# A weighted sum of expert outputs: twelve-token tiles in four buffers against sixteen-token tiles in three rooms

## The chip, the core and the metric

The kernel runs on one core of one Trainium2 chip. The metric is the device time of one execution in microseconds (us), the median of a few runs. The core has engines that compute, VectorE (DVE), ScalarE (ACT) and GpSimd (POOL), and SyncE (SP), which issues transfers. ACT and SP each issue transfers (DMAs) into a queue of their own, q10 and q1 in the profile; sixteen DMA engines serve both queues. TensorE (PE) has no work here.

## The reference

```python
batch, seq, hidden, n_experts, k = 16, 1024, 512, 8, 2
# expert_outputs: batch x seq x k x hidden, combine_weights: batch x seq x k, float32
def reference(expert_outputs, combine_weights):
    weights = combine_weights[..., np.newaxis]
    return np.sum(expert_outputs * weights, axis=2).astype(np.float32)
```

For each of 16,384 tokens, two rows of 512 numbers are scaled, each by its own weight, and added. A token is 4 KB of input and 2 KB of output: 67 MB are read and 33.5 MB written in all.

## The kernel before

The 16,384 tokens are spread over 128 partitions, 128 tokens each. The first 120 tokens of a partition are contiguous in memory (a pitch of 480 KB of input from one partition to the next, 240 KB of output); the last eight lie in a second block at the end of the tensors. `rows` (L34 to L38) hides that split.

The loop at L68 goes over eleven tiles: ten of 12 tokens and a last one of eight. Every tile takes one of four buffers of 12 tokens (`bufs=4`, 48 KB in each partition). Each tile is loaded by one DMA on SP (L75), so that a partition's part is one row of 48 KB; the first tile alone is cut into two tokens, moved in 4 KB rows, and ten. The result `ot` is written over the first half of the tile's own buffer, so that a buffer is free for the next load when its store has landed. SP therefore waits, before the load of tile g + 4, for the store of tile g.

There are three forms of the computation.

- Tiles 0 to 8: DVE alone multiplies the whole tile by its broadcast weights (L84), then adds the two halves (L85). ACT issues the store (L86).
- Tile 9: ACT scales the first half token by token (L92), DVE multiplies the second half (L107) and adds (L108). SP issues the store (L109).
- Tile 10, the last: token by token, ACT scales the first half (L92) and DVE does a multiply and add in one instruction (L96). SP issues the store.

Before all that ACT issues a small write of zeros to the output (`ahead`, L58), which the stores later cover, then the two loads of the weights (L62), and runs a one-element activation. The order on each engine is that of the program; a framework works out the semaphores for the waits. The queues serve their DMAs in order, and the sixteen DMA engines take from both queues.

Of the kernel before, what the change touches and what calls it, by code (L numbers as in the profile page):

```python
# [1 line left out]

# [4 lines left out]


@with_exitstack
def kernel(  # L10
    ctx: ExitStack,
    tc: tile.TileContext,
    expert_outputs: bass.AP,
    combine_weights: bass.AP,
    out: bass.AP,
):

    nc = tc.nc  # L20
    b, s, k, h = expert_outputs.shape
    assert k == 2
    n = b * s
    P = nc.NUM_PARTITIONS
    per = n // P
    assert per * P == n
    J, LAST = 12, 8
    main = per - LAST
    assert main % J == 0
    eo = expert_outputs.rearrange("b s k h -> (b s) (k h)")  # L30
    cw = combine_weights.rearrange("b s k -> (b s) k")
    o = out.rearrange("b s h -> (b s) h")

    def rows(x):  # L34

        a = x[0 : P * main, :].rearrange("(p t) f -> p t f", p=P)
        b = x[P * main : n, :].rearrange("(p t) f -> p t f", p=P)
        return lambda t, c: a[:, t : t + c, :] if t < main else b[:, t - main : t - main + c, :]  # L38

    eo, cw, o = rows(eo), rows(cw), rows(o)  # L40

    dt = mybir.dt.float32
    mult = mybir.AluOpType.mult
    add = mybir.AluOpType.add
    copy = mybir.ActivationFunctionType.Copy

    last = main // J

    wpool = ctx.enter_context(tc.tile_pool(name="w", bufs=1))
    ipool = ctx.enter_context(tc.tile_pool(name="in", bufs=4))  # L50

    wt = wpool.tile([P, per * k], dt)


    zt = wpool.tile([16, 128], dt)
    nc.vector.memset(zt, 0.0)  # L56
    first = out.rearrange("b s h -> (b s) h")[0 : P * main, :].rearrange("(q t) h -> q (t h)", q=16)
    ahead = nc.scalar.dma_start(out=first[:, 0:128], in_=zt)  # L58

    with tc.issue_after(ahead.ins):  # L60
        for t, c in ((0, main), (main, LAST)):
            nc.scalar.dma_start(  # L62
                out=wt[:, k * t : k * (t + c)].rearrange("p (t k) -> p t k", k=k), in_=cw(t, c)
            )
        warm = wpool.tile([P, 1], dt)
        nc.scalar.activation(out=warm, in_=nc.const_aps.tensor(1.0, (P, 1), dt), func=copy)  # L66

    for g in range(last + 1):  # L68
        et = ipool.tile([P, J, k * h], dt)

        ot = et.rearrange("p j f -> p (j f)")[:, 0 : J * h].rearrange("p (j f) -> p j f", f=h)
        t0, c = g * J, J if g < last else LAST

        for a, m in ((0, 2), (2, c - 2)) if g == 0 else ((0, c),):
            nc.sync.dma_start(  # L75
                out=et[:, a : a + m],
                in_=eo(t0 + a, m),
                max_dma_last_dim=k * h * 4 if g + a == 0 else None,
            )
        if g < last - 1:  # L80

            wb = wt[:, g * J * k : (g + 1) * J * k].unsqueeze(2).to_broadcast([P, J * k, h])
            ek = et.rearrange("p j (k h) -> p (j k) h", k=k)
            nc.vector.tensor_tensor(out=ek, in0=ek, in1=wb, op=mult)  # L84
            nc.vector.tensor_tensor(out=ot, in0=et[:, :, 0:h], in1=et[:, :, h : 2 * h], op=add)  # L85
            nc.scalar.dma_start(out=o(t0, c), in_=ot)  # L86
            continue


        for i in range(c):  # L90
            t = t0 + i
            nc.scalar.activation(  # L92
                out=et[:, i, 0:h], in_=et[:, i, 0:h], func=copy, scale=wt[:, 2 * t : 2 * t + 1]
            )
            if g == last:
                nc.vector.scalar_tensor_tensor(  # L96
                    out=ot[:, i, :],
                    in0=et[:, i, h : 2 * h],
                    scalar=wt[:, 2 * t + 1 : 2 * t + 2],
                    in1=et[:, i, 0:h],  # L100
                    op0=mult,
                    op1=add,
                )
        if g < last:
            w1 = wt.rearrange("p (t k) -> p t k", k=k)[:, t0 : t0 + c, 1:2]
            x1 = et[:, :, h : 2 * h]
            nc.vector.tensor_tensor(out=x1, in0=x1, in1=w1.to_broadcast([P, c, h]), op=mult)  # L107
            nc.vector.tensor_tensor(out=ot, in0=et[:, :, 0:h], in1=x1, op=add)  # L108
        nc.sync.dma_start(out=o(t0, c), in_=ot[:, 0:c])  # L109


# [1 line left out]
_INS = ['expert_outputs', 'combine_weights']  # L113
_OUTS = [((16, 1024, 512), 'float32')]


# [23 lines left out]
```

## Time and profile before

| what | value |
|---|---|
| runs | 239.13, 240.79, 239.16 us; median 239.16 |
| span of the profiled execution, first to last instruction | 237.34 us (no other time of that execution is listed) |
| median less that span | 1.82 us |
| DVE busy | 194.1 us in 29 instructions |
| ACT busy | 14.0 us in 22 instructions |
| moved | 100.80 MB in 3760 packets, 425 GB/s on the mean |
| load of 12 tokens, issue to landing | 29.9 us |
| store of 12 tokens on ACT's queue, issue to landing | 33.0 us |

A packet here is what a DMA engine moves in one go: the part of one partition in a DMA, 48 KB for a load of 12 tokens, 24 KB for its store. Each DMA of 128 partitions gives every one of the 16 engines eight packets. The DMA share is the busy time of the packets that start in a stretch, over 16 engines; in short stretches it swings, and can be over one, since a packet is counted whole where it starts.

### The profile page before, as it was taken

What the parts mean: (1) busy time and instruction counts of PE and PEld (TensorE: products, weight loads), DVE (VectorE), ACT (ScalarE), POOL (GpSimd) and SP (SyncE); (2) the same over time, 40 slices, a digit from 0 to 9 for tenths busy, and PEclk for the clock granted to TensorE, in tenths of its full rate; (3) what the DMA queues carried; (4) which work ended last, traced back from release to release, by engine and by line L of the source; (5) the groups of instructions that cost most, each with busy time, mean ns of one, the idle gap of its engine ahead of it and who ended that gap; (6) DMA issues with size and microseconds to landing.
All of it is one profiled execution on the core that took longest, in us unless ns stands there. A gap on an engine that the chain in (4) does not pass through costs nothing.

```text
span 237.3 us, 157 instructions
## 1 busy us (share of the span) xinstructions
DVE 194.1 (82%) x29; ACT 14.0 (6%) x22; POOL 0.2 (0%) x4
## 2 busy tenths in 40 slices
DVE  0008999999999999999999889969996998785710
ACT  2000000000000000000000000000000000740800
POOL 0000000000000000000000000000000000000000
DMA  7999999989899999999898999999998979999997
GB/s 289 452 474 398 398 448 480 398 356 505 352 443 435 427 464 464 398 398 530 348 514 348 447 418 443 464 464 398 398 522 348 522 344 451 464 398 442 406 434 309
DMA packets 3760, 100.80 MB, mean 425 GB/s; under 512 B 544, under 2 KB 688, under 8 KB 944
## 3 DMA queue, kind: packets, MB, share of 16 engines
q1 hardware_dynamic: 2144, 72.35, 71.0%
q10 hardware_dynamic: 1616, 28.45, 27.9%
HBM read 67.24 MB, written 33.56 MB: 425 GB/s over the span
## 4 chain that ended last, share of the span: by engine, by line
DMA 59%; DVE 34%; ACT 2%; ACTq 0%; DVEq 0%; issue 0%; SPq 0%
DMA out_dram<-et 29%; DMA et<-in_expert_outputs_dram 23%; DVE et L84 22%; DVE et L85 11%; DMA wt<-in_combine_weights_dram 7%; ACT et L92 2%; DVE et L96 1%; DVEq L135 0%; ACTq L135 0%; ACTq L58 0%; DVE zt L56 0%; DVEq L84 0%; SPq L75 0%; ACTq L92 0%
## 5 line engine op out<-in xcount | busy, mean ns | idle before, releaser
L84 DVE TENSOR_TENSOR et<-et,wt 128x12288 f32<-128x12288 f32 x9 | 116.6, 12955 | 24.1 <-DMA wt<-in_combine_weights_dram 17.5
L85 DVE TENSOR_TENSOR et<-et 128x6144 f32<-128x6144 f32 x9 | 59.0, 6557 | 0.3
L92 ACT ACTIVATE et<-et,wt 128x512 f32<-128x512 f32 x20 | 12.5, 708 | 208.6 <-DMA et<-in_expert_outputs_dram 208.6
L96 DVE SCALAR_TENSOR_TENSOR et<-et,wt 128x512 f32<-128x512 f32 x8 | 5.6, 746 | 3.9 <-ACT et L92 3.6
L107 DVE TENSOR_TENSOR et<-et,wt 128x6144 f32<-128x6144 f32 x1 | 6.6, 6557 | 2.3 <-DMA et<-in_expert_outputs_dram 2.3
L108 DVE TENSOR_TENSOR et<-et 128x6144 f32<-128x6144 f32 x1 | 6.6, 6558 | 0.9 <-ACT et L92 0.9
L66 ACT ACT_TABLE_LOAD x1 | 1.3, 1283 | 2.4 <-issue 2.4
L56 DVE MEMSET zt<- 16x128 f32 x1 | 0.2, 165 | 0.8 <-PEq L124 0.8
L66 ACT ACTIVATE warm<-const-float32-1.0 128x1 f32<-128x1 f32 x1 | 0.2, 202 | 0.0
L124 POOL MEMSET const-bfloat16-1.0<- 128x1 bf16 x1 | 0.1, 102 | 0.0
L124 POOL MEMSET const-uint8-127<- 128x1 uint8 x1 | 0.1, 101 | 0.0
L124 POOL MEMSET const-float32-0.0<- 128x1 f32 x1 | 0.1, 99 | 0.2 <-issue 0.2
L124 POOL MEMSET const-float32-1.0<- 128x1 f32 x1 | 0.1, 98 | 0.0
## 6 DMA issues: line engine op xcount, KB each, us to landing
et<-in_expert_outputs_dram SPq DMA_DIRECT2D x9, 6144.0 KB, 29.9
out_dram<-et ACTq DMA_DIRECT2D x9, 3072.0 KB, 33.0
et<-in_expert_outputs_dram SPq DMA_DIRECT2D x1, 5120.0 KB, 17.0
et<-in_expert_outputs_dram SPq DMA_DIRECT2D x1, 4096.0 KB, 25.1
out_dram<-et SPq DMA_DIRECT2D x1, 3072.0 KB, 14.6
out_dram<-et SPq DMA_DIRECT2D x1, 2048.0 KB, 10.0
et<-in_expert_outputs_dram SPq DMA_DIRECT2D x1, 1024.0 KB, 5.0
wt<-in_combine_weights_dram ACTq DMA_DIRECT2D x1, 120.0 KB, 17.0
```

What stands on the lines that cost most here:

```text
L56: nc.vector.memset(zt, 0.0)
L66: nc.scalar.activation(out=warm, in_=nc.const_aps.tensor(1.0, (P, 1), dt), func=copy)
L84: nc.vector.tensor_tensor(out=ek, in0=ek, in1=wb, op=mult)
L85: nc.vector.tensor_tensor(out=ot, in0=et[:, :, 0:h], in1=et[:, :, h : 2 * h], op=add)
L92: nc.scalar.activation(out=et[:, i, 0:h], in_=et[:, i, 0:h], func=copy, scale=wt[:, 2 * t : 2 * t + 1])
L96: nc.vector.scalar_tensor_tensor(out=ot[:, i, :], in0=et[:, i, h : 2 * h], scalar=wt[:, 2 * t + 1 : 2 * t + 2], in1=et[:, i, 0:h], op0=mul ...
L107: nc.vector.tensor_tensor(out=x1, in0=x1, in1=w1.to_broadcast([P, c, h]), op=mult)
L108: nc.vector.tensor_tensor(out=ot, in0=et[:, :, 0:h], in1=x1, op=add)
L124: nc = _bacc.Bacc("TRN2", target_bir_lowering=False, num_devices=1)
```

## The change

The kernel's schedule is written out by hand, in one function.

- Tiles are of 12, six times 16, 10 and 10 tokens. One tensor `et` holds three rooms of 16 tokens (64 KB in each partition each); tile g uses room g modulo 3, and its load is issued by SP behind the store of tile g - 3.
- Each tile is done token by token, in the form that only the last tile had (`WHOLE` and `MIXED` are empty): ACT scales one half, DVE multiplies and adds.
- The split of the tokens is moved: the first block has 12 tokens of each partition (48 KB of input pitch), the second block 116 (464 KB of input, 232 KB of output).
- The first tile is loaded as one token in a 4 KB row and 11 tokens. Its weights come by a small DMA on SP between the two; the other weights by one DMA on ACT.
- Stores 0 to 5 are issued by ACT. The results of tiles 6 and 7 (16 and 10 tokens) are written next to each other, the first at the top of its room and from its last token down (`up`), so that one DMA on SP stores 26 tokens as one row of 52 KB. The last tile's store follows on SP.

```diff
-    J, LAST = 12, 8
+    ROOM, ROOMS = 16, 3
+    TILES = [12, 16, 16, 16, 16, 16, 16, 10, 10]
+    FIRST = [1, 11, 16, 16]
+    STORES = [[0], [1], [2], [3], [4], [5], [6, 7], [8]]
+    WHOLE = []
+    MIXED = []
+    LAST = 116
     main = per - LAST
...
-    ipool = ctx.enter_context(tc.tile_pool(name="in", bufs=4))
+    et = pool.tile([P, ROOMS * ROOM, k * h], dt)
+    halves = et.rearrange("p j (k h) -> p (j k) h", k=k)
...
+    def combine(g, up):
+        at, c, t0 = g % ROOMS * ROOM, TILES[g], starts[g]
+        base = k * at + (k * ROOM - c if up else 0)
...
+        for i in range(c - 1, -1, -1) if up else range(c):
+            t = k * (t0 + i)
+            x0, x1 = halves[:, k * (at + i), :], halves[:, k * (at + i) + 1, :]
+            nc.scalar.activation(out=x0, in_=x0, func=copy, scale=wt[:, t : t + 1])
+            nc.vector.scalar_tensor_tensor(
+                out=halves[:, base + i, :], in0=x1, scalar=wt[:, t + 1 : t + 2], in1=x0, op0=mult, op1=add
             )
+        return base
...
+    with tc.manual_schedule():
+        nc.vector.memset(zt, 0.0)
+        ahead = flat[0 : P * main, :].rearrange("(q t) h -> q (t h)", q=16)
+        nc.scalar.dma_start(out=ahead[:, 0:128], in_=zt)
+        weights(nc.scalar, main, per - main)
...
+        t = 0
+        for i, c in enumerate(FIRST):
+            load(t, c, **({"max_dma_last_dim": k * h * 4} if i == 0 else {}))
+            t += c
+            if i == 0:
+                weights(nc.sync, 0, main)
+        for j, st in enumerate(STORES):
+            bases = [combine(g, up=len(st) == 2 and g == st[0]) for g in st]
+            c = sum(TILES[g] for g in st)
+            q = nc.sync if j in (6, 7) else nc.scalar
+            q.dma_start(out=o(starts[st[0]], c), in_=halves[:, bases[0] : bases[0] + c, :])
+            for g in st:
+                if g + ROOMS < len(TILES):
+                    load(starts[g + ROOMS], TILES[g + ROOMS])
```

`load` and `weights` issue one DMA each: a stretch of tokens into its place in `et`, and their weights into `wt`.

More of the change, by code (lines that the diff above doesn't have):

```diff
@@ L26 @@
     assert per * P == n
-    J, LAST = 12, 8
+    ROOM, ROOMS = 16, 3
[5 more added lines that the diff above has]
+    LAST = 116
+    assert sum(TILES) == per and [g for st in STORES for g in st] == list(range(len(TILES)))
     main = per - LAST
[L29 to L32, printed above, removed]
+    starts = [sum(TILES[:g]) for g in range(len(TILES))]
     def rows(x):
[L36 to L40, printed above, removed]
+        first = x[0 : P * main, :].rearrange("(p t) f -> p t f", p=P)
+        second = x[P * main : n, :].rearrange("(p t) f -> p t f", p=P)
+        return lambda t, c: first[:, t : t + c, :] if t < main else second[:, t - main : t - main + c, :]
+    flat = out.rearrange("b s h -> (b s) h")
+    eo = rows(expert_outputs.rearrange("b s k h -> (b s) (k h)"))
+    cw = rows(combine_weights.rearrange("b s k -> (b s) k"))
+    o = rows(flat)
     dt = mybir.dt.float32
@@ L45 @@
     copy = mybir.ActivationFunctionType.Copy
-    last = main // J
-    wpool = ctx.enter_context(tc.tile_pool(name="w", bufs=1))
-    ipool = ctx.enter_context(tc.tile_pool(name="in", bufs=4))
[L52 to L63, printed above, removed]
-            )
-        warm = wpool.tile([P, 1], dt)
-        nc.scalar.activation(out=warm, in_=nc.const_aps.tensor(1.0, (P, 1), dt), func=copy)
@@ L68 @@
[L68 to L109, printed above, removed]
@@ new lines, with place, load @@
+    pool = ctx.enter_context(tc.tile_pool(name="all", bufs=1))
+    et = pool.tile([P, ROOMS * ROOM, k * h], dt)
+    halves = et.rearrange("p j (k h) -> p (j k) h", k=k)
+    wt = pool.tile([P, per * k], dt)
+    wk = wt.rearrange("p (t k) -> p t k", k=k)
+    zt = pool.tile([16, 128], dt)
+    warm = pool.tile([P, 1], dt)
+    def place(t):
+        g = max(g for g in range(len(TILES)) if starts[g] <= t)
+        return g % ROOMS * ROOM + t - starts[g]
+    def load(t, c, **kw):
+        at = place(t)
+        assert place(t + c - 1) == at + c - 1
+        nc.sync.dma_start(out=et[:, at : at + c], in_=eo(t, c), **kw)
@@ new lines, in weights @@
+    def weights(q, t, c):
+        q.dma_start(out=wk[:, t : t + c, :], in_=cw(t, c))
+    def combine(g, up):
+        at, c, t0 = g % ROOMS * ROOM, TILES[g], starts[g]
+        base = k * at + (k * ROOM - c if up else 0)
+        if g in WHOLE or g in MIXED:
+            assert not up
+            room = halves[:, k * at : k * (at + c), :]
+            x0, x1 = et[:, at : at + c, 0:h], et[:, at : at + c, h : 2 * h]
+            if g in WHOLE:
+                wb = wt[:, k * t0 : k * (t0 + c)].unsqueeze(2).to_broadcast([P, k * c, h])
+                nc.vector.tensor_tensor(out=room, in0=room, in1=wb, op=mult)
+            else:
+                for i in range(c):
+                    x = et[:, at + i, 0:h]
+                    nc.scalar.activation(out=x, in_=x, func=copy, scale=wt[:, k * (t0 + i) : k * (t0 + i) + 1])
+                w1 = wk[:, t0 : t0 + c, 1:2].to_broadcast([P, c, h])
+                nc.vector.tensor_tensor(out=x1, in0=x1, in1=w1, op=mult)
+            nc.vector.tensor_tensor(out=halves[:, base : base + c, :], in0=x0, in1=x1, op=add)
+            return base
[5 more added lines that the diff above has]
+                out=halves[:, base + i, :], in0=x1, scalar=wt[:, t + 1 : t + 2], in1=x0, op0=mult, op1=add
+            )
+        return base
@@ new lines @@
+    with tc.manual_schedule():
[3 more added lines that the diff above has]
+        weights(nc.scalar, main, per - main)
+        nc.scalar.activation(out=warm, in_=nc.const_aps.tensor(1.0, (P, 1), dt), func=copy)
+        t = 0
[4 more added lines that the diff above has]
+                weights(nc.sync, 0, main)
+        assert t == sum(TILES[:ROOMS])
+        for j, st in enumerate(STORES):
+            bases = [combine(g, up=len(st) == 2 and g == st[0]) for g in st]
+            c = sum(TILES[g] for g in st)
+            assert bases[-1] == bases[0] + sum(TILES[g] for g in st[:-1])
+            q = nc.sync if j in (6, 7) else nc.scalar
[3 more added lines that the diff above has]
+                    load(starts[g + ROOMS], TILES[g + ROOMS])
```

## The prediction

> **What bounds the kernel now.** I read the page first: its span, the busy tenths, the DMA line and the packets. Then I asked for busy time by stretches, then for the waits of SP's queue, and last for the timeline of the end.
>
> ```profile
> span 237.3 us, 157 instructions
> DVE 194.1 (82%) x29; ACT 14.0 (6%) x22; POOL 0.2 (0%) x4
> ...
> DMA  7999999989899999999898999999998979999997
> ...
> DMA packets 3760, 100.80 MB, mean 425 GB/s; under 512 B 544, under 2 KB 688, under 8 KB 944
> ...
> DMA out_dram<-et 29%; DMA et<-in_expert_outputs_dram 23%; DVE et L84 22%; DVE et L85 11%; DMA wt<-in_combine_weights_dram 7%; ACT et L92 2%; DVE et L96 1%; DVEq L135 0%; ACTq L135 0%; ACTq L58 0%; DVE zt L56 0%; DVEq L84 0%; SPq L75 0%; ACTq L92 0%
> ```
>
> The DMA engines are full from the first slice to the last. The chain of waits puts a third of the span on DVE (L84, L85), and that invites the wrong conclusion: it only says which event released the next one. The stretches settle it (columns: length, busy time by engine, clock, DMA share, GB/s):
>
> ```profile
> 0.00:4.00 4.00, 0.17 (x1) 1.49 (x2) 0.20 (x4) 1.00 0.52 158
> ...
> 38.00:50.00 12.00, 12.00 (x2) 0.00 (x0) 0.00 (x0) 1.00 0.94 387
> 50.00:230.00 180.00, 162.46 (x26) 12.47 (x20) 0.00 (x0) 1.00 1.00 432
> 230.00:237.34 7.34, 0.00 (x0) 0.00 (x0) 0.00 (x0) 1.00 0.78 333
> ```
>
> From 50 to 230 us the DMA share is 1.00 at 432 GB/s, while DVE is busy 162.46 of 180 us. Counting each packet's bytes over its own duration rather than at its start, I get 433.4 GB/s there. So bytes are the bound, and DVE is second. The trace's packet records tell where the rest goes. The first packet starts at 1.79 us; the last ends at 236.14, lands at 236.49, and the span ends at 237.34. In between, 100.8 MB at 433.4 GB/s would be 232.6 us, and 234.35 passed. Of the 1.75 us lost, about 0.75 is the cold start (16 packets of 4 KB per engine, 159 ns each, would end at 4.33 us; on the mean they end near 5.1, single ones having taken up to 1071 ns), 0.57 is load packets of 1815 ns that took up to 2331 ns around the first store (0.32 at 41 us, 0.25 at 47), and the rest is small.
>
> Packets have a fixed cost: 24,576 B take 912 ns and 49,152 B take 1815 ns, so a byte costs 0.03674 ns on one of 16 engines and a packet 9 ns besides.
>
> ```profile
> SPq L75 <- DMA out_dram<-et: 174.1, 7, 45.8
> ```
>
> SP, which issues the loads, waits 174.1 us for stores to free a buffer (total, times, longest), and yet the queues never run dry, because other loads are still in flight. The timeline of the end (start, length) prices the token-wise form:
>
> ```profile
> 219.90 5.01 ACT L92 ACTIVATE et<-et,wt 128x512 f32<-128x512 f32 x8 [9.48 <-DMA et<-in_expert_outputs_dram]
> 220.66 5.78 DVE L96 SCALAR_TENSOR_TENSOR et<-et,wt 128x512 f32<-128x512 f32 x8 [3.65 <-ACT et L92]
> ```
>
> Eight tokens take 5.78 us on DVE, 0.7225 us each, behind a first scaling on ACT (0.76 us from 219.90 to 220.66).
>
> **The change, part by part.**
>
> *Computation.* DVE loses nine pairs of 12.955 + 6.557 us and the pair L107, L108 (13.1 us), and has 128 token steps instead of eight: 128 x 0.7225 = 92.5 us for 194.1. ACT gets 128 scalings of 0.626 us (5.01 / 8), 80 us. Load to store becomes 0.76 + 16 x 0.7225 = 12.3 us for a tile of 16, 9.4 for the 12, 8.0 for a 10; it was 19.5 us for 12. Worth to the end: nothing, since it lies beside full DMA engines. The cover is the covers below.
>
> *ACT's queue.* Each store waits for DVE's last token, with the next tile's scalings behind it. DVE trails by at most 16 x (0.7225 - 0.626) + 0.72 = 2.3 us. The next tile's data comes much later (a turn of 16 tokens is 29 us, below), so nobody waits.
>
> *Packets.* Before: loads 1664, stores 1408, weights 256, the early zeros 16, and 16 completion words for each of 26 DMAs (416), together the page's 3760. After: loads 10 x 128 = 1280, stores 8 x 128 = 1024, weights 256, zeros 16, completions 21 x 16 = 336, together 2912. That is 848 fewer at 9 ns over 16 engines: -0.47 us. No row shows a packet of 65,536 B (the largest is 49,152). If a 64 KB row goes as two packets, 768 come back and the gain is 0.04 us. I take one packet, as every row up to 48 KB went.
>
> *Start.* SP issues one token, the 96-byte weights, then 11 tokens. Issues are 0.47 us apart (0.725, 1.199), so the 11 tokens are issued at about 1.67 and can start 1.07 us later (0.725 to 1.79), at 2.74. One token in 4 KB packets is 8 x 0.159 = 1.27 us from 1.79, so at full rate it lasts to 3.06: covered by 0.3 us, which is also the price if it is not. The weights' 128 packets cost between 11 ns (the 64 B row) and 44 ns (960 B) each, at most 0.35 us; the 64 B packets that go give 0.09 back. Fewer 4 KB packets could spare up to half of the cold 0.75. These are of opposite sign and I take 0, between -0.4 and +0.6.
>
> *Three rooms.* A load of 16 is eight 64 KB packets per engine, by the slope 2.417 us each; its store is eight of 32 KB at 1.213 us (the 32 KB row). With both queues taking turns a tile is 8 x 3.63 = 29.0 us. Tile 0 has landed at about 17.6 and is computed at 26.6; the first store packet comes 5.1 us later (as 38.04 to 43.1 before), at 31.7. Then 10.2 load packets are left; eight pass beside store 0 (8 x (2.417 + 0.912) = 26.6 us), which lands at 58.7, when load 3 is issued. Still queued: 2.2 load packets beside store 1, 8.0 us of work against the 1.07 that the new load needs. Each later store takes eight turns to eight load packets, so the lead stays. Before, the same lead is 8.2 us (load issued at 107.63, the one ahead landed at 115.79). Cost 0.
>
> *The end.* When store 5 lands, 2.2 packets of load 7 (ten tokens) are left, 2.2 x 1.514 (the 40 KB row) = 3.3 us, for 1.07. Load 8 then is 12.1 us, and covers tile 7: landing 0.35, computing 8.0, store issue 1.07, together 9.5; 2.6 us to spare. The joint store is eight packets of 52 KB, 1.965 each, 15.7 us, and covers tile 8 (9.4 us). It waits on SP behind load 8, and only the last store is behind it. Cost 0.
>
> *Pitch.* Input rows are 464 KB apart instead of 480, output rows 232 instead of 240. At 480 the load packets of 48 KB are at 1815 ns from 50 us on: no loss to win back. Below: 0. Above: the nearest rows are the stretched packets around the first store; if each of the eight stores paid 0.57 us, that is 4.6, less the 0.57 that is paid already, +4.0; if each paid half, +1.7. I take 0, as the ten later stores stretched nothing that can be seen.
>
> A rule speaks against long regular pitches: the Trainium skill, "DMA: Bandwidth & Descriptors", section "Latency and other measured facts", has copies at a row pitch of 512 KiB at 207 GB/s per direction where 214 is full. By it, were 464 KB as bad, the sum would be 3.4% of 232.6 us, 7.9 us, higher, an estimate of 246.6 us. This trace, at 480 KB, shows no such loss, and no run here shows 512.
>
> **Sum.** 237.34 - 0.47 = 236.87 us of span. The three runs' median lies 239.16 - 237.34 = 1.82 us above this span; the profiled execution has no other time listed, so I add 1.82 and stand against the median: 238.7 us.
>
> **The rivals.**
>
> *Two packets for a 64 KB row.* For it: nothing that large in the trace. Against: one descriptor for each row so far. 237.34 - 0.04 + 1.82 = 239.1.
>
> *The end runs dry: slower.* Place: between load 8 and the joint store. It decides once a token costs more than 0.98 us (2.6 us over ten tokens), and each 0.1 us beyond adds 1 us. For it: alternate steps wait on DVE itself, and scalings on ACT, and 128 in a row have not been seen. Against: the eight seen had the same waits at 0.7225. At 1.25 us a token: 2.7 us, 241.4.
>
> *The pitch slows HBM: slower.* From 1.2% longer packets (2.8 us) it is over a per cent. Price 240.4 to 242.7 (the +1.7 and +4.0 above). For it: both pitches are new. Against: 480 shows nothing, and the rows are longer.
>
> *The losses of start and first stores go: faster.* 0.75 + 0.57 = 1.3 us, 237.4. Faster than that has a floor in bytes alone: 100.8 MB x 0.03674 / 16 = 231.5, plus 1.79 and 1.20 and 1.82, 236.3. Against: cold start and first store are still there.
>
> **How the numbers follow.** Forecast 0.70, two packets 0.08, dry end 0.08, pitch 0.08, losses gone 0.06. About 1% (2.4 us) is what a measurement of this kernel can tell from no change: 236.8 to 241.5. Faster 0.03 (half of the last case, if still more goes); slower 0.14 (nearly all of the two slow cases); within 0.83. The likeliest case's own range is 238.3 to 239.3, by the start's bounds. The range for 8 in 10 takes in the losses gone (237.4) and a dry end or a pitch of up to 2.8 us: 237.4 to 241.5.
>
> **What would show it.** Right: the DMA share stays 1.00 from 50 to 230 us at 433 GB/s; about 2912 packets, the 64 KB ones at 2.42 us; DVE near 92 us busy and idle more than half; a load always issued several us before the load ahead lands. Wrong: 3680 packets (two to a row); a DMA share under 0.97 around 198 or 210 us (dry end); packets over 2.45 us in the middle (pitch). The forecast fails if token steps cost nearer 1 us, or packets stretch.

## The result, and the profile after

The changed kernel takes 241.76 us (median of four runs: 241.0, 241.0, 242.5, 242.8) against 239.16 before: a ratio of 1.0101, 95% interval 1.007 to 1.0133. It is slower by a per cent; 238.7 was forecast, 237.4 to 241.5 as the range. The runs lie in two pairs, one 1.8 us above the kernel before and one 3.4 and 3.7.

The page of the profiled execution (the longest of the four: 242.82 us, of which 241.03 are the span):

```profile
span 241.0 us, 417 instructions
DVE 87.4 (36%) x129; ACT 81.0 (34%) x130; POOL 0.2 (0%) x4
...
DMA  8999979979999998989999998989998999999992
...
DMA packets 2915, 100.83 MB, mean 418 GB/s; under 512 B 464, under 2 KB 608, under 8 KB 736
...
q14 instruction: 3, 0.02, 0.0%
```

DVE's work is more than halved, and the DMA engines look as full as before. Two things are new: three packets of a queue q14 "instruction", and a last slice at 2 tenths. The stretches show where the difference lies. Before, then after (columns: stretch, length, busy DVE, ACT and POOL, clock, DMA share, GB/s):

```profile
50.00:195.00 145.00, 138.11 (x16) 0.00 (x0) 0.00 (x0) 1.00 1.00 434
195.00:236.00 41.00, 24.35 (x11) 12.47 (x20) 0.00 (x0) 1.00 0.98 422
236.00:241.00 5.00, 0.00 (x0) 0.00 (x0) 0.00 (x0) 1.00 0.00 0
```

```profile
50.00:195.00 145.00, 55.86 (x83) 51.06 (x83) 0.00 (x0) 1.00 1.01 435
195.00:236.00 41.00, 17.23 (x26) 13.99 (x23) 0.00 (x0) 1.00 0.98 421
236.00:241.00 5.00, 0.00 (x0) 0.00 (x0) 0.00 (x0) 1.00 0.12 49
```

The computation is as forecast, and the waits of SP's queue keep their form (timeline of tile 1, then the wait of the loads):

```profile
43.13 9.91 ACT L99 ACTIVATE et<-et,wt 128x512 f32<-128x512 f32 x16 [16.19 <-DMA et<-in_expert_outputs_dram]
43.89 11.08 DVE L100 SCALAR_TENSOR_TENSOR et<-et,wt 128x512 f32<-128x512 f32 x16 [15.46 <-ACT et L99]
55.00 0.34 ACTq L125 DMA_DIRECT2D out_dram<-et  x1
```

```profile
SPq L72 <- DMA out_dram<-et: 178.0, 6, 39.5
```

Sixteen tokens take 11.08 us on DVE, and ACT issues the store right behind; SP waits 178.0 us for stores, as it waited 174.1 before.

Up to 236 us, by the stretches, the two kernels move data alike. Then the kernel before is done, while in the changed one there is a share of 0.12 until 241 us, as much as two of the sixteen DMA engines would give if they worked all that time. A few engines are late, not all of them. The trace shows it directly: it has sixteen completions for every DMA, one for each DMA engine. Here is how far the last of them comes behind the median one, in us, with the median engine's end of the last store:

```
                 tile 0   tile 1   tile 2   store 5   load 8   last store   median engine's end
before            0.26     0.26     0.21     0.23      0.21      0.19         236.29
changed           1.77     2.28     2.27     2.25      3.61      3.59         236.44
```

Before, all sixteen stay within 0.3 us from start to end. In the changed kernel one engine is 1.8 us late when tile 0 has landed, never recovers, and is 3.6 us late at the end (the packets tell that it is the same one: each starts where the one before it on its engine ends). A second engine is 1.2 us late with tile 0 and 2.3 at the end. Of the 3.54 us by which the last landing moved (236.49 to 240.03), 0.15 is the median engine's and 3.40 the growth of the spread. Each DMA gives every engine its fixed eight rows, so no other takes work off a late one.

### The profile page after: what moved, and what is told of

The parts are those of the page before. It is cut to its first block, busy times and chain, and to the rows that moved or that the text cites. A ratio compares the mean times of both kernels' runs of the same rounds, so it can differ in the third digit from the quotient of the medians.

```text
span 241.0 us, 417 instructions
## 1 busy us (share of the span) xinstructions
DVE 87.4 (36%) x129; ACT 81.0 (34%) x130; POOL 0.2 (0%) x4
## 2 busy tenths in 40 slices
DMA packets 2915, 100.83 MB, mean 418 GB/s; under 512 B 464, under 2 KB 608, under 8 KB 736
## 4 chain that ended last, share of the span: by engine, by line
DMA 81%; DVE 6%; ACT 5%; issue 1%; SPq 0%; DVEq 0%; ACTq 0%
DMA et<-in_expert_outputs_dram 41%; DMA out_dram<-et 40%; DVE et L100 6%; ACT et L99 5%; DVEq L154 0%; ACTq L154 0%; SPq L72 0%; SPq L75 0%; ACTq L99 0%; DVEq L100 0%
## 5 line engine op out<-in xcount | busy, mean ns | idle before, releaser
L100 DVE SCALAR_TENSOR_TENSOR et<-et,wt 128x512 f32<-128x512 f32 x128 | 87.2, 747 | 138.4 <-ACT et L99 136.7
L99 ACT ACTIVATE et<-et,wt 128x512 f32<-128x512 f32 x128 | 79.5, 708 | 141.7 <-DMA et<-in_expert_outputs_dram 140.3
```

Of the source, the lines that this page charges most:

```text
L99: nc.scalar.activation(out=x0, in_=x0, func=copy, scale=wt[:, t : t + 1])
L100: nc.vector.scalar_tensor_tensor(out=halves[:, base + i, :], in0=x1, scalar=wt[:, t + 1 : t + 2], in1=x0, op0=mult, op1=add)
```

## The experiments

The theories, by the letters used below. I: instructions fetched by the DMA engines while the kernel runs make single engines late. S: the start does, through the small weights rows between the first two loads (S1) or through a first load too short to cover the second's issue (S2). E: the 16 us without a store near the end stretch the late engines' load packets. R: three rooms leave the load queue too short a lead. P: the pitch. Q, which came later: small weights DMAs hold ACT's queue. Their main rival at first: the token-wise form is free, and only start and end cost anything.

Lag below means that measure: last of the sixteen completions less the median one. Ratios are to the kernel before, on the same chip.

**More instructions in the kernel before** (`b_tiny`).

```diff
             nc.scalar.dma_start(out=o(t0, c), in_=ot)
+            for r in range(14):
+                nc.scalar.activation(out=tiny[:, r : r + 1], in_=ot[:, r % J, 0:1], func=copy)
+                nc.vector.tensor_copy(out=tiny[:, 16 + r : 17 + r], in_=ot[:, r % J, 1:2])
             continue
```

> The kernel before, with 14 one-column copies on DVE and 14 on ACT added behind each of its first nine tiles (their results are not used). Theory I (instruction transfers: a longer program makes the engines fetch instructions by DMA while the kernel runs, 8 KB at a time, each taking 0.3 us on one DMA engine and stretching the packet after it by 0.25 to 0.53 us, and that engine then ends last): packets of queue 14 appear in the middle, one to three of them, one or two DMA engines end 0.6 to 1.6 us behind the others, the time is 239.6 to 240.8 us. Rival (only the start and the end of the changed kernel cost anything): no change, 239.2 us.

239.71 us against 239.11, ratio 1.0025 (1.0015 to 1.0035). Two instruction packets of 8 KB appear, at 99.7 and 105.1 us; each takes 0.309 us, and a load packet that follows is stretched by 0.53 and 0.24. The lag rises from 0.2 to 0.8 us, while the median engine ends as before (236.27). Stores 1 to 7 are issued 0.7 to 3.5 us later than in the kernel before, and the median engine doesn't feel it. Theory I holds: the two transfers fell on two engines, which are 0.9 and 0.6 us late at the next landing, and the later one sets the time.

**Every tile token by token, else as before** (`b_tokenwise`).

```diff
-        if g < last - 1:
...
-            nc.vector.tensor_tensor(out=ek, in0=ek, in1=wb, op=mult)
-            nc.vector.tensor_tensor(out=ot, in0=et[:, :, 0:h], in1=et[:, :, h : 2 * h], op=add)
         for i in range(c):
...
-            if g == last:
-                nc.vector.scalar_tensor_tensor(
+            nc.vector.scalar_tensor_tensor(
```

> The kernel before with its tiles, buffers, start and stores, but every tile done token by token. Theory I: as many instructions as in the changed kernel, so about three instruction transfers and 0.6 to 1.6 us on the DMA engine that gets them, 239.6 to 240.8 us. Rival: the token-wise form is free, since DVE has 92 us of work for 194, 239.2 us.

242.48 us, ratio 1.0139 (1.0124 to 1.0154): both expectations missed. There are three transfers (84, 106, 219 us). The lag goes from 0.2 to 2.0 us after the first, since the load packets that follow on its engine are stretched too (by 0.54, 0.60 and 0.20 us), and to 2.9 after the third; the second fell on another engine (0.5 us late). What is lost shows at the end, where the lag is gone:

```profile
217.00:231.00 14.00, 4.28 (x8) 3.84 (x7) 0.00 (x0) 1.00 0.98 421
231.00:235.00 4.00, 2.69 (x5) 1.17 (x2) 0.00 (x0) 1.00 0.20 84
235.00:241.00 6.00, 0.00 (x0) 0.00 (x0) 0.00 (x0) 1.00 0.72 306
```

The queues run dry for some 3.5 us (a share of 0.20) before the last store. With a fast computation the stores go out early and take their turns from the loads, so the last load lands on the median engine at 224.2 us in place of 219.6. On the last engine it lands 2.9 us after that, at 227.1, and only then do its 6.6 us of computation begin; no store is left to cover them. So the slow DVE of the kernel before was a cover, not a burden, and the late engine took away what cover was left. An estimate from these numbers: had all engines landed together, at 224.3, the last store would have been issued 2.7 us earlier, and under 1 us of the 3.5 would have been dry.

**Fewer DVE instructions in the changed kernel** (`a_mixed`: `MIXED = [0, 1, 2, 3, 4, 5]`).

> The changed kernel with tiles 0 to 5 computed by ACT token by token and two large DVE instructions a tile. Theory I: DVE's instructions fall below what fills its first pages and ACT's stay, so one or two of the three instruction transfers go, the slowest DMA engine gains at most 0.8 us, 240.2 to 242 us. Rival (the start decides): DMA engines that start late by 1 to 2 us stay the last ones, no change within 0.4 us. A loss of over 1 us would mean that the later stores (17.5 us a tile in place of 12.3) let the queues run dry.

244.46 us, ratio 1.022 (1.0193 to 1.0247). One transfer fewer, and worse: a tile takes 18.7 us from its landing to its store where the changed kernel has 12.0, the stores are later, load 8 is issued at 203.2 us in place of 200.2, and the queues run short (share 0.90, 369 GB/s from 195 to 215 us). The third outcome named there came.

**The changed kernel again** (`a_again`, no edit).

> The changed kernel once more, for a second profile. If the late DMA engines at the start are a matter of chance, other engines are late, or none, and the time is 241.0 or 242.5 us accordingly; the three instruction transfers (at 80, 90 and 225 us) and the stretched packets around 30, 202 and 214 us come again in every execution.

241.69 us, ratio 1.0115 (1.009 to 1.014), single runs 240.98 to 243.05. The transfers come again at 80.1, 89.6 and 223.6 us, the stretches around 30, 202 and 214 us too, and the lag at tile 0 is 1.66, at the end 2.80. The stretch around 202 us is larger here, 0.5 us on the mean of the engines for 0.1, and the median engine ends 0.9 us later than before too (237.21 for 236.29). So the last landing is again 3.5 us late, but only 2.6 of it are the growth of the lag.

**The start of before** (`a_start`).

```diff
-    FIRST = [1, 11, 16, 16]
+    FIRST = [2, 10, 16, 16]
+        weights(nc.scalar, 0, main)
         weights(nc.scalar, main, per - main)
-            if i == 0:
-                weights(nc.sync, 0, main)
```

> The changed kernel with the start of before: two tokens in 4 KB rows, then ten, and the weights of tile 0 on ACT's queue, ahead of the others. Theory S (two DMA engines began the 11-token rows at 5.6 and 6.2 us where the others began at 3.9 to 4.4, behind small weights packets that took 0.3 us in place of 0.04, and stay last to the end): all engines begin the ten-token rows within 0.6 us, tile 0 lands by 18.3 us in place of 20.1, the runs lie together, near 240.0 us; what stays is the instruction transfers and the end. Rival (the 48 KB pitch of tile 0 makes the start slow): engines still late by over 1 us, 241 to 242.5 us.

241.59 us, ratio 1.0096 (1.0078 to 1.0113), single runs 241.45 to 241.72. The start is even (lag 0.37 at tile 0) and the runs lie together, as theory S has it; the time is not what it said. A new loss shows in the timeline (start, length; in brackets the idle time before and what ended it):

```profile
27.43 0.35 ACTq L124 DMA_DIRECT2D out_dram<-et  x1
37.88 9.91 ACT L99 ACTIVATE et<-et,wt 128x512 f32<-128x512 f32 x16 [12.19 <-DMA wt<-in_combine_weights_dram]
```

Tile 1 waits for its weights until 37.9 us, and the trace's packets show that store 0, issued at 27.4, starts only at 39.5. Loads run out at 64.5 us, only stores move until 69.4, and around that start the packets are stretched by 1.4 us on the mean of the engines.

**Another pitch** (`a_pitch`).

```diff
-    LAST = 116
+    LAST = 10
-        weights(nc.scalar, main, per - main)
+        weights(nc.scalar, 12, main - 12)
+        weights(nc.scalar, main, per - main)
-                weights(nc.sync, 0, main)
+                weights(nc.sync, 0, 12)
```

> The changed kernel with the split of the tokens at 118 in place of 12: tiles 0 to 7 at a pitch of 472 KB, the last tile at 40 KB, the weights of tile 0 still by a small DMA on SP. Theory S (order of the small weights DMAs): the start stays uneven, 241 to 242.5 us. Rival P (the 48 KB pitch of the first block, or 464 KB of the second): the first 45,056-byte packets take 1665 ns, the start is even, 239.5 to 240.5 us.

242.89 us, ratio 1.0147 (1.0118 to 1.0176), runs 241.8 to 243.9, over both ranges; lag 1.2 at tile 0, so the start stays uneven, as theory S has it. Packets of 64 KB take 2.42 us at 472 KB as at 464, so neither pitch costs anything. On two engines the second weights DMA on ACT comes late: it lands at 37.1 us on the last, at 18.2 on the median one. Store 0 behind it lands at 63.7 on the last (59.6 in the changed kernel), load 8 is issued at 203.1, and the loads run dry there (share 0.79 from 195 to 206 us).

**Tile 6 stored by itself** (`a_stores`: `STORES = [..., [5], [6], [7], [8]]`, the last two on SP).

> The changed kernel with tile 6 stored by itself on ACT in place of one store of 26 tokens with tile 7. Theory E (the 16 us without any store, 198 to 214 us, stretch load packets at their end on the engines that are late): the stretched packets at 214 us go, up to 1.5 us on the slowest engine. But the store of tile 6 then runs beside load 8, which lands some 9 us later, and the store of ten tokens left behind it (6 us) does not cover the 9 us until the last store can start: the queues run dry for about 3 us near 230 us. Together 242 to 244 us. Rival (the joint store hides nothing): 240.0 us.

244.61 us, ratio 1.022 (1.0198 to 1.0242). As theory E has it, no packet is stretched at 202 or 214 us, and the lag at load 8 is 2.2 us (3.4 at load 7) where the changed kernel has 3.6; and as expected the end is dry:

```profile
217.00:229.00 12.00, 1.46 (x2) 2.69 (x5) 0.00 (x0) 1.00 0.97 420
229.00:235.00 6.00, 5.43 (x9) 3.55 (x6) 0.00 (x0) 1.00 0.09 39
```

Six us with a share of 0.09, where three were expected; load 8 lands 2.2 us late on the last engine, and the last store waits for it. So the joint store is worth its place.

**Both** (`a_both`: the start of before and the store of tile 6 by itself).

> The changed kernel with the start of before and tile 6 stored by itself. By theories S and E: an even start and a dry end, 241.5 to 243 us, all DMA engines ending within 1 us of each other but for the instruction transfers. If the two parts do not add up, one of them is read wrongly.

244.48 us, ratio 1.0218 (1.0195 to 1.024), above the range. The two parts add up in time (241.59 + 244.61 - 241.76 = 244.44): an even start, lag 0.13, and a dry end, with the dry loads at 64 us, which the expectation did not have.

**Only the weights moved** (`a_wact`: one token, then eleven, both weights DMAs on ACT).

> The changed kernel with its first load of one token kept, and the weights of tile 0 moved from SP's queue to ACT's, ahead of the others. Theory S1 (the small weights rows on SP, between the two first loads, make two DMA engines late): the start is even as with the start of before, spread of the 16 engines at the landing of tile 0 under 0.5 us. Theory S2 (one token is too little to cover the issue of the second load, so ACT's 928-byte rows get through first and are slow on some engines): the spread stays at 0.8 to 1.8 us and the times of single runs stay 241 to 243 us.

242.38 us, ratio 1.0129 (1.0113 to 1.0144), runs 242.1 to 242.5. Lag at tile 0 0.46 and no variation: S1, not the single token. Store 0 again starts 10 us late (29.4 to 39.7), and the loads are dry at 64 us.

**Four rooms of 12, token by token** (`a_4x12`).

```diff
-    ROOM, ROOMS = 16, 3
-    TILES = [12, 16, 16, 16, 16, 16, 16, 10, 10]
-    FIRST = [1, 11, 16, 16]
-    STORES = [[0], [1], [2], [3], [4], [5], [6, 7], [8]]
-    LAST = 116
+    ROOM, ROOMS = 12, 4
+    TILES = [12] * 10 + [8]
+    FIRST = [2, 10, 12, 12, 12]
+    STORES = [[0], [1], [2], [3], [4], [5], [6], [7], [8, 9], [10]]
+    LAST = 8
+        weights(nc.scalar, 0, main)
-                weights(nc.sync, 0, main)
```

> The hand-written schedule and the token-wise form with four rooms of 12, ten tiles of 12 and one of 8, the start and the 480 KB pitch of before, tiles 8 and 9 stored as one row. Theory R (three rooms of 16 leave the load queue so short a lead that an engine 1 to 2 us ahead of the slowest runs dry): no packet is stretched between 60 and 230 us but at instruction transfers, the median engine ends at 236.2 us as before, the last one 1 to 2 us later by the instruction transfers, time 239.8 to 241.2 us. Rival (the three rooms are as good, all is start and instructions): the same 241.5 us as the changed kernel with the start of before.

241.69 us, ratio 1.0103 (1.009 to 1.0117). Nothing runs dry from 60 to 210 us, the lag goes from 0.2 to 1.8 us after the transfer of 84 us (the one of 92 fell on another engine, 0.5 us late); but the joint store is issued at 218.3, after the last load has landed on most engines (216.9), and the share is 0.65 from 217 to 220. All engines wait there, and the lag is gone at the end (0.07). It is paid all the same: the joint store waits for tile 9, which lands 1.8 us later on the last engine than on the median one. So the run doesn't decide on the rooms: it has a dry end of its own.

**The same with few instructions** (`c_4x12w`: `WHOLE = [0, ..., 7]`, `MIXED = [9]`).

> As the four rooms of 12, but tiles 0 to 7 as two large DVE instructions each and tile 9 in the mixed form, so few instructions. Theory I: no instruction transfer in the middle, the 16 engines end within 0.5 us, time 239.0 to 239.4 us, as before. Rival (the joint store, or the hand order, costs something): over 239.8 us with even engines.

240.47 us, ratio 1.0064 (1.004 to 1.0087). No transfer in the middle, and the sixteen engines stay within 0.26 us all the way: theory I. The time is the rival's: the joint store at 217.0 comes too late again.

```profile
216.00:219.00 3.00, 1.99 (x3) 1.83 (x3) 0.00 (x0) 1.00 0.62 262
```

**One token first, in the kernel before** (`b_first1`: `((0, 1), (1, c - 1))` for `((0, 2), (2, c - 2))`).

> The kernel before with one token of 4 KB rows in its first load in place of two, and eleven in the next. Theory S2 (one token does not cover the second load's issue): the engines are unequal from the start on, the landing of tile 0 spreads by over 0.5 us, the time rises by 0.5 to 2 us and varies. Theory S1: even, 239.1 us (8 packets of 4 KB fewer on each engine, under 0.1 us).

239.87 us, ratio 1.0029 (1.002 to 1.0038). Tile 0 lands evenly (lag 0.26) but the packets at the first store are stretched by 1.4 us on the mean of the engines, for 0.57 before. Neither theory had that.

**The weights split between the queues otherwise** (`d_wsp`).

```diff
-    FIRST = [1, 11, 16, 16]
+    FIRST = [2, 10, 16, 16]
-        weights(nc.scalar, main, per - main)
+        weights(nc.scalar, 0, main)
-            if i == 0:
-                weights(nc.sync, 0, main)
+            if i == 1:
+                weights(nc.sync, main, per - main)
```

> The changed kernel with two tokens and then ten in its first load, the weights of tile 0 on ACT and the other weights on SP, behind the load of tile 0 and ahead of that of tile 1. Theory Q (with both weights DMAs on ACT, as with the start of before, their 16 packets per engine each wait a turn behind a 64 KB load packet, so ACT's queue is taken until 37.5 us and store 0, issued at 27.4, starts at 39.5; the loads then run dry at 64 us and starting again costs 1.4 us): store 0 starts 4 to 7 us after its issue, load 3 is issued by 60 us, nothing is stretched at 64 to 72 us, the 16 engines land tile 0 within 0.5 us, and the time is 239.6 to 240.6 us: the forecast of 238.7 plus the delay of one engine by the instruction transfers (0.9 to 1.9 us). Rival (the three rooms run dry whatever the start): store 0 early, but packets stretched by a microsecond at 64 to 72 us again, 241.5 us.

241.42 us, ratio 1.0091 (1.0061 to 1.0121), runs 240.95 to 242.65. Theory Q holds: store 0 starts at 32.3 us, 4.9 after its issue, load 3 is issued at 57.4, nothing is stretched at 64 to 72 us, tile 0 lands with a lag of 0.19. The size was too small. The engine that ends last has a lag of 0.9 after the transfer at 79.7 us, 1.6 by 128 us (four more of its load packets are stretched, by 0.14 to 0.33 us each, without a transfer), 2.4 at load 8 and 3.1 after the transfer at 222.4, while the median engine ends at 236.25. The transfer at 85.9 fell on another engine, which is 0.8 us late.

**And more instructions in that** (`d_tiny`).

```diff
+            if j < 6:
+                for r in range(20):
+                    nc.scalar.activation(out=tiny[:, r : r + 1], in_=nc.const_aps.tensor(1.0, (P, 1), dt), func=copy)
+                    nc.vector.memset(tiny[:, 32 + r : 33 + r], 0.0)
```

> The same with 20 one-column instructions on ACT and 20 on DVE behind each of tiles 0 to 5 (their results are not used), which take 1 to 5 us of engines that are idle for 17 us a tile. Theory I: three or so instruction transfers more in the middle, the last of the 16 engines falls 0.5 to 1.5 us further behind the median one, the time rises by as much. Rival (instruction transfers only matter where the queues are short anyway): within 0.3 us of the kernel without them.

244.09 us, ratio 1.0194 (1.017 to 1.0218), 2.7 us more than without, and above the 0.5 to 1.5 expected. Page of that run:

```profile
q14 instruction: 5, 0.04, 0.0%
```

Five transfers, two more. The lag is 0.2 before those at 54 and 57 us and 1.9 by 88 us, 3.2 after the one at 140, 4.2 at the end, 1.1 more than without; the median engine is 0.9 us later. (The two profiled executions are 2.0 us apart.) Store 5 lands on the last engine at 200.9 us, 3.2 after the median, and only then is load 8 issued, when most engines have 1 us of load 7 left. So a late engine also starves the others.

**The changed kernel's start in the kernel before** (`b_wsp`: one token, the 96-byte weights rows on SP, eleven tokens; the others on ACT).

> The kernel before with the changed kernel's start: one token of 4 KB rows, the 96-byte weights rows of tile 0 on SP, then eleven tokens; all else as before. Theory S1 (the small weights rows on SP between the first two loads make one or two DMA engines late): the 16 engines land tile 0 with the last one 0.7 to 1.8 us behind the median, the lag stays to the end, the single runs vary by a microsecond, 239.9 to 241.5 us. Rival (one token alone did it, or the hand-written order): as even as with one token and the weights on ACT (last 0.3 us behind the median), 239.9 us without variation.

240.16 us, ratio 1.0034 (1.0015 to 1.0053), runs 239.05 to 241.01. The variation came with it, for 0.4 us with one token and the weights on ACT. The place was not as expected: in the profiled execution tile 0 lands evenly (0.30), and a lag of 2.4 us, 1.5 at the end, comes at the first store.

No version that was run beats the kernel before.

## Why the prediction was wrong, point by point

The step that failed is one that several terms share: the sum reckons with one DMA engine for all sixteen, and so puts what happens to single engines at nothing ("Worth to the end: nothing", "I take 0", "Cost 0"). In the profiled execution the median engine has its last landing at 236.44 us, near what the sum gives (236.49 less 0.47). The last engine comes 3.6 us behind it: 1.8 us from the start, 0.5 from the first store, 1.3 from load 8. This is one execution, the longest; the two of 241.0 us were not traced.

- **The bound: right.** 435 GB/s from 50 to 195 us, and 2915 packets, the 2912 counted and three instruction packets. A 64 KB row goes as one packet, of 2418 ns (2417 by the slope). The pitch costs nothing.
- **The work of DVE and ACT: right in size** (87.4 and 81.0 us for 92.5 and 80; 0.69 us a token; 12.0 us from tile 1's landing to its store, 12.3 forecast). **"Worth to the end: nothing" was wrong, as other kernels show.** It priced the token-wise form in engine time and not in instructions. A longer program is fetched by the same DMA engines while the kernel runs: two transfers alone cost 0.6 us in the kernel before, two more cost 2.7 us with three rooms. Where the start is even (`d_wsp`), two of the three fall on the engine that ends last and make 1.5 of its 3.1 us of lag; stretched packets behind the first make 0.8, load 8 makes 0.7. In the changed kernel's own profiled execution the transfers fell on engines that were not the last, so there they add nothing to the end. Lags of different engines don't add up, the largest counts: with an even start the transfers take its place, and the time falls by 0.3 us only (241.42 for 241.76), less than the runs of either kernel vary.
- **The packets, -0.47 us: mis-sized.** 9 ns a packet is its duration, but the records of neighbouring packets on an engine overlap by about 4 ns; measured, the rate from 50 to 195 us is 433.6 GB/s by the packets' own durations where it was 433.5 before, 0.1 us over the whole.
- **"Start ... I take 0": wrong.** The sum reckoned with one DMA engine for all sixteen. The median engine has tile 0 0.4 us later (18.31 for 17.92), inside the bounds given; the last one has it 1.9 us later (20.08 for 18.18), having begun its eleven-token rows at 6.2 us where most began between 3.9 and 4.4. The first store belongs here too: the packets around it are stretched by 0.45 us on the mean of the engines, about as reckoned, but by 0.9 on the late one.
- **Three rooms, "Cost 0": right for the lead.** Load 3 was issued at 59.7 (58.7 forecast), with 8.6 us of the median engine's loads still ahead (8.0). (In the sum 17.6 us and 9.4 of computing for tile 0 make 27.0, not 26.6; store 0 was issued at 28.5.) It held only because ACT's queue was free; with both weights DMAs on it, it didn't (`a_start`, `a_wact`).
- **"The end ... Cost 0": wrong.** Load 8 was issued at 200.2, when the median engine had 2.3 us to the landing of load 7, for the 3.3 reckoned, since store 5 lands 2.3 us later on the last engine. Two engines ahead ran dry (for 1.1 and 0.6 us), and the late ones were stretched while the others began the joint store. The dry-end rival had this place but the wrong cause: tokens got cheaper (0.69 us), not dearer.
- **The rule on pitches** from the Trainium skill, "DMA: Bandwidth & Descriptors", section "Latency and other measured facts", is on large powers of two, of which 512 KiB is the least in its list, not on long pitches as such. It didn't decide: 464, 472 and 480 KB run alike here, at 433 to 434 GB/s from 50 to 195 us, and no run has 512.

What stays open: no run has three rooms with an even start and few instructions, so the split of the last engine's 3.6 us is read from one trace and not confirmed by taking all its parts away at once. Open too is why a weights DMA on SP goes with times that vary. Of all kernels here, each that has one varied from run to run by 0.7 to 2.1 us, and without one the runs lie within 0.4 us but for rare single ones; a late engine can arise at the first small packets (the changed kernel) or at the first store (`b_wsp`). It isn't known either why load packets of an engine that is already late are stretched again with no transfer before them (`d_wsp`). Not tried: the joint store with tile 6 cut smaller, which might keep stores moving beside load 8 without a dry end.

## What to carry to other kernels

When the DMA engines are full, ask for the last of them, not for their mean: each has its own rows, so a microsecond lost on one stays lost until all engines wait, and every wait for a landing passes it on. A compute form that is cheaper in engine time can cost more in instructions, which are fetched over the same DMA engines; and a slow engine behind full queues may be the cover of the tail, so before you speed it up, look at what is left to move when the last load has landed. Keep queues free of small DMAs ahead of the first store, since each small packet waits a turn behind a big one.

## What the runs showed of the hardware

- Instruction transfers: 8 KB packets of queue 14, 0.309 us each; three with 208 DVE and 153 ACT sequencer instructions, two with 174 and 178 (`b_tiny`), none during the work with 48 and 52. With the stretch of the load packet behind it, 0.24 to 0.54 us, one brings its DMA engine 0.5 to 0.9 us behind at once, and 1.4 to 1.8 by the next landing where more load packets behind it are stretched (`a_4x12`, `b_tokenwise`).
- Two queues share the DMA engines packet by packet, and the turn doesn't look at size: 16 weights packets of 96 and 928 B per engine, which take 0.43 us by themselves (12 and 42 ns each), held ACT's queue until 37.5 us behind load packets of 1.5 and 2.4 us (`a_start`).
- Going from reads alone to reads and writes stretches the load packets under way by 0.4 to 1.4 us on the mean of the engines (0.45 at 30 us in the changed kernel, 0.57 around 41 us before, 1.4 in `b_first1`), and starting loads again after a stretch of stores alone costs 1.4 us (`a_start`).
